# A hybrid mixer block on one core: inverses beside the other branches, key phases beside them without priority, gates beside the recurrence

## The chip, the core and the metric

The kernel runs on one core of a Trainium2 chip. The metric is the device time of one execution in microseconds. TensorE (PE in the profile) multiplies matrices, VectorE (DVE) and ScalarE (ACT) do elementwise work, GpSimd (POOL) does little but issue DMAs here, and SyncE (SP) issues the weight loads.

## The reference

One layer of a sequence model: 512 frames (`S`), width 1024, one batch. The input goes through an RMS norm and one wide projection. Its columns feed three mixers, which are gated, added and projected back; an MLP with squared ReLU and a final norm follow.

```
h = rms_norm(x, norm1_g);  p = h @ w_in
y_a = b_a * causal_dwconv(c_a * x_a)                       # short gated convolution
y_b = rg_lru(causal_dwconv(x_b)) * gelu(g_b)               # gated linear recurrence
r, decay, k, v, kk, a = ...                                # RWKV-7: keys, values, decays
state = state * w_t + (state @ -kk_t) (kk_t * a_t) + v_t k_t ;  y_t = state @ r_t
y_c = (norm(y) * lnx_g + lnx_b + bonus) * g_c
m = gate_a * y_a + gate_b * y_b + gate_c * y_c             # gates: sigmoid(p_g + bias)
x = x + m @ w_out
x = x + square(relu(rms_norm(x) @ w1)) @ w2 ;  out = rms_norm(x)
```

The third mixer has 16 heads of 64 and runs in eight chunks (`CHUNK = 64`) whose state is carried on.

## The kernel before

**Precision.** Every projection is computed from fp32 values split into a high and a low part. `load_w` fetches one 128x1024 weight block on SP's queue into `raw` (two buffers), ScalarE makes the high part `whi`, VectorE the low part `wlo`, and `mm3` (L165 to L168) does three matmuls per contraction block, 24 per block of 128 output columns (`proj`).

**Phase 1, four groups `g` of four heads.** `krv(g)` projects keys, receptances and values, builds the decays and the operands `AR` and `BK` of the chunk-internal products, and stores some of them to DRAM. `amat(g)` multiplies `BK` with `AR` for every chunk (tiles `pA`, L522), masks the products on VectorE into `AXt`, transposes `BK` (`pB`) and stores. `inverse(g)` solves a triangular system per chunk and head: 31 steps of two VectorE operations on the tiles `dg` and `Z`, with transposes ahead (L549) and behind (L566, L571), then two blocks of 32-wide matmuls (`pG`, `pT`) and the store `ttd`.

**Other branches.** `ab(q)`, for eight column blocks `q`, is mixer A and mixer B of 128 columns: eight projections, small gate matmuls (`pga`, `pgi`), ScalarE functions and a VectorE scan. It yields 32 times and stores its part of `m` to `mpd`. `gate(q)` is the third mixer's gate: the projection `gc`, the small matmul `pg2` with the low-rank gate, and the merge with `mpd` (read back as `yc` on POOL's queue).

**Phase 2, the recurrence.** `chain()` goes through eight chunks. Each has three dependent blocks of 64-wide matmuls (`pu` from the state, `pu` again with the inverse, `pS` for the next state) with copies on VectorE and ScalarE between, and the outputs `py`. `load_chunk` fetches the operands (`sv`, `ax`, `tc`, `bk`, `rt`) of the next chunk on POOL's queue into two buffers each. After every second chunk `norm` normalises two chunks of output, on VectorE for the most part.

**Phase 3.** `fin_m` transposes four chunks of output (`pYt`), multiplies them with the gate and splits the sum into `mh` and `ml`; `w_out(th)` is the output projection of one half of the frames (tiles `acc`, then `x2T`, `h2h`, `h2l`). Then come the MLP's two matrices (tiles `p` and `acc`) and the final norm.

**What sets the order.** The kernel is written in generators, and a scheduler with its own idea of durations places each engine's instructions by priority. `weave(crit, fill, r)` advances a critical generator and, after each of its steps, the filler by `r` steps on average. What the critical one emits gets a priority offset: `CP = 150` unless it yields another number (`CPI`, `CPC`, `CPN`). `pin` keeps small blocks of matmuls together on PE. In phase 1 the critical generators are `krv(0)` and `amat(0)`, and then, for each later group, `krv(g)` and `inverse(g-1)` step by step side by side, followed by `amat(g)`; the filler is `ab`. In phase 2 the chain is critical with 3.9 filler steps to each of its own; the filler is the rest of `ab`, then the gates, then `fin_m(0, 4)` and `w_out(0)`. `end()` does `fin_m(4, 8)`; what then remains of the filler, `w_out(1)` and the MLP follow.

Of the kernel before, what the change touches and what calls it, by code (L numbers as in the profile page):

```python
# [18 lines left out]
P = 128  # L19

OFF, OFFS, OFFP = 160, 20, 30
CP, CPI, CPC, CPN = 150, 60, 70, 5
HOT = 6000

NINV, NG_T = 16, 2


N_AB = 28
R0, R1, R2, R3, R4 = 0.85, 0.60, 1.25, 3.9, 1.0
NWARM = 2  # L30
POOL_KT = (1, 3, 5, 6, 7)
S = 512
# [3 lines left out]
KT = 8  # L36
NG = 4
# [59 lines left out]
def block_kernel(ctx, tc, xt, win, par, mulr, sw, wout, w1, w2, fg, cst, eyes, out):  # L97
# [415 lines left out]
    def amat(g, G_):  # L513

        G_.AX = p1.tile([P, 2, NC, 4, L], F32, tag="AXt", name="AXt")
        for c4 in range(2):
            pts = four_banks("pA")
            for i in range(16):
                ci, jj, h = i // 4, i // 2 % 2, i % 2
                c = 4 * c4 + ci  # L520
                rows = slice(64 * h, 64 * h + 64)
                pin(i, lambda: pe.matmul(pts[2 * h + jj][:, ci], G_.BK[rows, jj, c], G_.AR[rows, jj, c],  # L522
                                 start=True, stop=True))
            for e in range(4):
                tt(G_.AX[:, :, 4 * c4:4 * c4 + 4, e], pts[e].rearrange("p c (a t) -> p a c t", a=2),
                   mask.rearrange("p (a t) -> p a t", a=2).unsqueeze(2).to_broadcast([P, 2, 4, L]), MUL)
            yield
        gp.dma_start(axd[:, 0:64, g, 1].rearrange("c s e t -> s c (e t)"),
                     G_.AX[0:64, 1].rearrange("s c e t -> s c (e t)"))
        for a in range(2):  # L530
            gp.dma_start(axd[:, 64:128, g, a].rearrange("c s e t -> s c (e t)"),
                         G_.AX[64:128, a].rearrange("s c e t -> s c (e t)"))
        BKT = p1.tile([P, NC, 2, P], F32, tag="BKT", name="BKT")
        for c2, pt in enumerate(four_banks("pB")):
            for i in range(4):
                c, jj = 2 * c2 + i // 2, i % 2
                pin(c2 + i, lambda: pe.transpose(pt[:, i], G_.BK[:, jj, c].rearrange("p a t -> p (a t)"), ident))
            ac.copy(BKT[:, 2 * c2:2 * c2 + 2].rearrange("p c j t -> p (c j) t"), pt)
        gp.dma_start(bkd[:, :, g].rearrange("c p j x -> p c (j x)"), BKT.rearrange("p c j x -> p c (j x)"))
        yield  # L540

    def inverse(g, G_):
# [35 lines left out]
            ac.copy(gs[32:64, 16 * half:16 * half + 16], pg[32:64])  # L578
            yield
        for _ in range(NG_T):  # L580
            yield CPI
        for half in range(2):
            pg = pm.tile([P, 16, 32], F32, tag="pm", name="pT")
            for i in range(16):
# [31 lines left out]

    def chain():
        nxt = load_chunk(0)
        yield CPC
        for c in range(NC):  # L620
            ax, sv, tc_, rt, bk = nxt
            if c < NC - 1:
# [185 lines left out]
        for x_ in gens:  # L808
            yield from x_

    def weave(crit, fill, r):
        acc, cp = 0.0, CP
        while True:
            with tc.high_priority(offset=cp):
                c = next(crit, weave)
            if c is weave:
                break
            cp = CP if c is None else c
            acc += r
            while acc >= 1.0:  # L820
                acc -= 1.0
                next(fill, None)

    def side_by_side(*gens):
        live = list(gens)
        end = object()
        while live:
            for x_ in list(live):
                c = next(x_, end)
                if c is end:  # L830
                    live.remove(x_)
                else:
                    yield c

    M = {}
    wk_ctx = ExitStack()
    wk = wk_ctx.enter_context(tc.tile_pool(name="wk", bufs=1, side="right"))
    GS = [G() for _ in range(NG)]
    fl = chainit(*[ab(q) for q in range(6)])
    weave(chainit(krv(0, GS[0]), amat(0, GS[0])), fl, R0)  # L840
    for g in range(1, NG):
        weave(chainit(side_by_side(krv(g, GS[g]), inverse(g - 1, GS[g - 1])), amat(g, GS[g])), fl, R1)
    weave(inverse(NG - 1, GS[NG - 1]), fl, R2)
    pk_ctx.close()
    p1_ctx.close()
# [10 lines left out]

    def fill_chain():
        yield from fl
        for q in (6, 7):
            yield from ab(q)  # L860
        for q in range(KT):
            yield from gate(q)
        wk_ctx.close()
# [225 lines left out]
```

## Time and profile before

| what | us |
|---|---|
| median of 3 runs (1158.6 to 1161.83) | 1159.1 |
| the profiled execution | 1160.24 |
| its span, first to last instruction | 1158.1 |
| PE busy / DVE busy / ACT busy in it | 1073.4 / 758.3 / 484.8 |
| first inverse, from its first transpose | 107.0 |
| last transpose of the fourth inverse | 538.5 |
| first matmul of the recurrence | 564.66 |
| first matmul of the MLP | 799.4 |

The span is the profile's time from the first to the last instruction; the execution's own time is 2.1 us longer. A busy engine is not an engine at its peak: PE's matmuls are pipelined, their ends are modelled, and a matmul that waits in the pipe counts as busy. So work on PE is better counted in instructions: 90 wide matmuls of 512 columns pass in 20 us of the MLP. Counts from a trace can be a few per cent low.

### The profile page before, as it was taken

To read this page: it belongs to the slowest core of one execution; us is meant where nothing else is said; L and a number is where in the kernel's file an instruction comes from. 1 tells how busy PE (TensorE), PEld (TensorE's weight loads), DVE (VectorE), ACT (ScalarE), POOL (GpSimd) and SP (SyncE) were. 2 spreads that over 40 slices of the span, in tenths; PEclk is the share of its full clock that TensorE was granted. 3 is DMA by queue.
4 is the path that set the end of the run, shared out by engine and by line. 5 is a ranking of instruction groups with operands and counts; after the bars stand their busy time and mean duration, and the time that the engine had idled before them with its cause. 6 is when DMAs were issued, how large, how long until landed. Compare 5 with 4: busy or idle time off the path is not lost.

```text
span 1158.1 us, 16176 instructions
## 1 busy us (share of the span) xinstructions
PE 1073.4 (93%) x6396; PEld 877.3 (76%) x6396; DVE 758.3 (65%) x1300; ACT 484.8 (42%) x714; POOL 108.6 (9%) x167
## 2 busy tenths in 40 slices
PE   8899898998899788996999999969999999999997
PEld 5677676876677566785788888868888888888885
DVE  7997998599957996697375767877444444222224
ACT  6645443544345343543364644535443343121123
POOL 4211000010001000100211120000000000000001
PEclk9999898998999888897999999979999999999999
DMA  6344533362236322361865474426322334333331
GB/s 206 96 126 109 140 94 110 101 172 86 84 109 173 96 77 97 91 169 60 261 214 169 155 217 146 165 91 196 114 91 93 107 92 156 133 93 91 104 97 72
DMA packets 44475, 146.32 MB, mean 126 GB/s; under 512 B 5808, under 2 KB 9392, under 8 KB 43376
## 3 DMA queue, kind: packets, MB, share of 16 engines
q1 hardware_dynamic: 30624, 95.21, 25.9%
q0 software_dynamic: 13056, 49.03, 14.9%
q8 instruction: 50, 0.82, 0.3%
q10 hardware_dynamic: 720, 1.05, 0.2%
q14 instruction: 25, 0.20, 0.1%
HBM read 120.11 MB, written 25.17 MB: 125 GB/s over the span
## 4 chain that ended last, share of the span: by engine, by line
PE 48%; DVE 4%; DMA 3%; issue 1%; ACT 1%; POOL 0%; ACTq 0%; POOLq 0%; DVEq 0%
PE acc L167 5%; PE acc L166 5%; PE acc L168 5%; PE p L168 5%; PE p L166 5%; PE p L167 5%; PE pp L168 4%; PE pp L167 4%; PE pp L166 4%; DMA raw<-in_wout 1%; PE py L642 1%; ACT whi L145 1%; DVE wlo L102 1%; DMA raw<-in_w 1%; DMA bk<-bkd 1%
## 5 line engine op out<-in xcount | busy, mean ns | idle before, releaser
L102 DVE TENSOR_TENSOR wlo<-raw,whi 128x1024 fp32r<-128x1024 f32 (+1 forms) x172 | 209.1, 1217 | 290.6 <-ACT whi L145 289.5
L145 ACT CAST whi<-raw 128x1024 fp32r<-128x1024 f32 (+1 forms) x172 | 177.8, 1036 | 359.4 <-PE pp L167 137.3
L166 PE MATMUL pp<-hh,whi 128*128 128x512 f32 x696 | 280.1, 406 | 19.2 <-DVE ks L105 10.2
L167 PE MATMUL pp<-hl,whi 128*128 128x512 f32 x696 | 282.0, 406 | 3.2 <-DVE hl L105 3.2
L168 PE MATMUL pp<-hh,wlo 128*128 128x512 f32 x696 | 281.7, 406 | 1.9 <-DVE wlo L102 1.9
L166 PEld LDWEIGHTS pp<-hh,whi 128*128 128x128 f32 x696 | 135.8, 195 | 52.3 <-DVE ks L105 11.5
L167 PEld LDWEIGHTS pp<-hl,whi 128*128 128x128 f32 x696 | 135.6, 195 | 33.4 <-DVE hl L105 4.0
L168 PEld LDWEIGHTS pp<-hh,wlo 128*128 128x128 f32 x696 | 136.1, 196 | 31.2 <-DVE wlo L102 2.3
L168 PE MATMUL p<-h2h,wlo 128*128 128x512 f32 (+1 forms) x264 | 101.1, 383 | 0.0
L166 PE MATMUL p<-h2h,whi 128*128 128x512 f32 (+1 forms) x264 | 101.1, 383 | 0.0
L167 PE MATMUL p<-h2l,whi 128*128 128x512 f32 (+1 forms) x264 | 101.0, 383 | 0.0
L166 PE MATMUL acc<-whi,ah 128*128 128x512 f32 x256 | 99.6, 389 | 0.0
L167 PE MATMUL acc<-wlo,ah 128*128 128x512 f32 x256 | 99.6, 389 | 0.0
L168 PE MATMUL acc<-whi,al 128*128 128x512 f32 x256 | 99.6, 389 | 0.0
L167 PEld LDWEIGHTS p<-h2l,whi 128*128 128x128 f32 x264 | 49.6, 188 | 9.7
L168 PEld LDWEIGHTS p<-h2h,wlo 128*128 128x128 f32 x264 | 49.6, 188 | 9.7
L166 PEld LDWEIGHTS p<-h2h,whi 128*128 128x128 f32 x264 | 49.6, 188 | 9.5
L166 PEld LDWEIGHTS acc<-whi,ah 128*128 128x128 f32 x256 | 48.0, 188 | 10.1
L167 PEld LDWEIGHTS acc<-wlo,ah 128*128 128x128 f32 x256 | 48.0, 188 | 10.1
L168 PEld LDWEIGHTS acc<-whi,al 128*128 128x128 f32 x256 | 48.0, 188 | 9.8
L102 DVE TENSOR_TENSOR Z<-Z,dg 64x31 f32<-64x31 f32 (+15 forms) x124 | 42.2, 340 | 4.0
L102 DVE TENSOR_TENSOR dg<-Z 64x31 f32<-64x31 f32 (+15 forms) x124 | 42.2, 340 | 3.9
(296 smaller groups left out, 1479.2 us busy)
## 6 DMA issues: line engine op xcount, KB each, us to landing
raw<-in_win SPq DMA_DIRECT2D x88, 512.0 KB, 3.5
raw<-in_w SPq DMA_DIRECT2D x64, 512.0 KB, 3.5
ax<-axd POOLq DMA_DIRECT2D x8, 1024.0 KB, 8.0
raw<-in_wout SPq DMA_DIRECT2D x16, 512.0 KB, 3.5
axd<-AXt POOLq DMA_DIRECT2D x12, 512.0 KB, 7.2
bkd<-BKT POOLq DMA_DIRECT2D x4, 1024.0 KB, 13.9
bk<-bkd POOLq DMA_DIRECT2D x7, 512.0 KB, 4.5
swr<-in_sw SPq DMA_DIRECT2D x16, 128.0 KB, 2.5
```

Of the source, the lines that this page charges most:

```text
L102: return v.tensor_tensor(out=o, in0=a, in1=b, op=op)
L145: ac.copy(hi[:, sl], raw[:, sl])
L166: pe.matmul(ps, wh, xh, start=start, stop=False)
L167: pe.matmul(ps, wh, xl, start=False, stop=False)
L168: pe.matmul(ps, wl, xh, start=False, stop=stop)
L642: pin(behind, lambda: pe.matmul(py[64 * h:64 * h + 64, x], w, y, start=first and x == 0, stop=last, skip_group_check=True))
```

## The change

Phase 1 is woven in turn instead of side by side. For each later group, first `inverse(g-1)` is critical with 29 filler steps spread over its 41, then `krv(g)` with priority offset 0 and 14 filler steps over its 22, then five filler steps alone, then `amat(g)` with one filler step to each of its own. All eight `ab` are in the filler from the start. The last inverse has 0.8 filler steps to each of its own (before 1.25), the chain 1.6 (before 3.9). In `inverse` the 4 steps (before 2) between its two blocks of matmuls have priority 0; the chain's own priority goes from 70 to 20 and six steps (before one) follow the first chunk load. `amat` starts each chunk with the second head pair. No instruction is added or removed.

```diff
-CP, CPI, CPC, CPN = 150, 60, 70, 5
+CP, CPI, CPK, CPC, CPN = 150, 60, 0, 20, 5
 HOT = 6000
-NINV, NG_T = 16, 2
-N_AB = 28
-R0, R1, R2, R3, R4 = 0.85, 0.60, 1.25, 3.9, 1.0
+NINV, NG_T, N_LOAD = 16, 4, 6
+N_INV, N_KRV = 41, 22
+F_INV, F_KRV, F_GAP = 29, 14, 5
+R0, R2, R3, R4 = 0.85, 0.8, 1.6, 1.0
...
-                ci, jj, h = i // 4, i // 2 % 2, i % 2
+                ci, jj, h = i // 4, 1 - i // 2 % 2, i % 2
...
         for _ in range(NG_T):
-            yield CPI
+            yield 0
...
         nxt = load_chunk(0)
-        yield CPC
+        for _ in range(N_LOAD):
+            yield CPC
...
-    def weave(crit, fill, r):
-        acc, cp = 0.0, CP
+    def weave(crit, fill, r, base=CP):
+        acc, cp = 0.0, base
...
-            cp = CP if c is None else c
+            cp = base if c is None else c
...
-    def side_by_side(*gens):
-        live = list(gens)
-        end = object()
-        while live:
-            for x_ in list(live):
-                c = next(x_, end)
-                if c is end:
-                    live.remove(x_)
-                else:
-                    yield c
...
-    fl = chainit(*[ab(q) for q in range(6)])
-    weave(chainit(krv(0, GS[0]), amat(0, GS[0])), fl, R0)
-    for g in range(1, NG):
-        weave(chainit(side_by_side(krv(g, GS[g]), inverse(g - 1, GS[g - 1])), amat(g, GS[g])), fl, R1)
+    fl = chainit(*[ab(q) for q in range(KT)])
+    weave(krv(0, GS[0]), fl, R0)
+    for g in range(NG):
+        if g:
+            weave(inverse(g - 1, GS[g - 1]), fl, F_INV / N_INV)
+            weave(krv(g, GS[g]), fl, F_KRV / N_KRV, CPK)
+            for _ in range(F_GAP):
+                next(fl, None)
+        weave(amat(g, GS[g]), fl, 1.0)
     weave(inverse(NG - 1, GS[NG - 1]), fl, R2)
...
         yield from fl
-        for q in (6, 7):
-            yield from ab(q)
         for q in range(KT):
             yield from gate(q)
```

What this does to the order shows at three places. In the changed file the helpers' lines are one higher (L102 becomes L103).

The first place is VectorE in the middle of the first inverse. `Z` and `dg` are its own; `a`, `AR` and `BK` belong to the keys of group 1, `wlo` is a low weight part, `u` and `g` belong to the branches. Before:

```order
L102 TENSOR_TENSOR Z<-Z,dg 64x14x18
L102 TENSOR_TENSOR wlo<-raw,whi 128x1024
L105 SCALAR_TENSOR_TENSOR BK<-a_1267,a_1263 128x8x64
L108 TENSOR_SCALAR a_1270<-a_1255,part,dv 128x512
L102 TENSOR_TENSOR dg<-Z 64x255
L102 TENSOR_TENSOR a_1270<-a_1270,ks 128x512
L102 TENSOR_TENSOR Z<-Z,dg 64x15x17
L102 TENSOR_TENSOR BK<-a_1270,a_1263 128x8x64
L102 TENSOR_TENSOR dg<-Z 64x256
```

With the change:

```order
L103 TENSOR_TENSOR Z<-Z,dg 64x14x18
L103 TENSOR_TENSOR wlo<-raw,whi 128x1024
L103 TENSOR_TENSOR dg<-Z 64x255
L106 SCALAR_TENSOR_TENSOR u_1187<-u_1138,part,u_1187 128x511
L103 TENSOR_TENSOR Z<-Z,dg 64x15x17
L106 SCALAR_TENSOR_TENSOR u_1187<-u_1138,part,u_1187 128x510
L103 TENSOR_TENSOR dg<-Z 64x256
L106 SCALAR_TENSOR_TENSOR u_1187<-u_1138,part,u_1187 128x509
L103 TENSOR_TENSOR Z<-Z,dg 64x16x16
```

The key operations have left the inverse: between its first and last transposes stood 76 operations of other tiles and 11 weight splits in the first group, and now 14 and 7.

The second place is PE in the recurrence, around the second block `pu` of a chunk. `pp` is a projection (of a branch before, of a gate now), `pg` the small gate matmul. Before, in the third chunk:

```order
L167 MATMUL pp<-hl,whi 128x512
L168 MATMUL pp<-hh,wlo 128x512
L166 MATMUL pp<-hh,whi 128x512
L652 MATMUL pu<-u_5033,tc 64x64 x16
L167 MATMUL pp<-hl,whi 128x512
L168 MATMUL pp<-hh,wlo 128x512
```

With the change, in the fourth:

```order
L167 MATMUL pp<-hh,whi 128x512
L168 MATMUL pp<-hl,whi 128x512
L169 MATMUL pp<-hh,wlo 128x512
L654 MATMUL pu<-u_5433,tc 64x64 x16
L167 MATMUL pg_5466<-lgh,swch 128x512
L168 MATMUL pg_5466<-lgl,swch 128x512
L169 MATMUL pg_5466<-lgh,swcl 128x512
```

Before, 22 projection matmuls stood between that chunk's two `pu` blocks and 23 between the second and `pS`; now it is 8 and 8, and 3 of `pg`. Over the recurrence up to its last `pS` the projection matmuls go from 475 to 211, and ahead of the recurrence from 1673 to 1896.

The third place is PE at the recurrence's end. `pYt` are the transposes of `fin_m`, `acc` is the output projection. Before:

```order
L702 MATMUL pYt<-ident,Y 128x128 x4
L632 MATMUL pu<-sv,ax 64x64 x16
L642 MATMUL py<-St,rt 64x64 x16
L702 MATMUL pYt<-ident,Y 128x128 x8
L166 MATMUL acc<-mh,whi 128x256 x3
L167 MATMUL acc<-ml,whi 128x256
```

With the change, 27 matmuls after the last `py` of the last chunk:

```order
L167 MATMUL pg_6345<-lgh,swch 128x512
L168 MATMUL pg_6345<-lgl,swch 128x512
L169 MATMUL pg_6345<-lgh,swcl 128x512
L704 MATMUL pYt<-ident,Y 128x128 x12
L167 MATMUL acc<-mh,whi 128x256 x3
L168 MATMUL acc<-ml,whi 128x256
```

Before, the first half's output projection began between the last chunk's first `pu` block and its second; now all of it follows the last chunk.

## The prediction

> **What bounds the kernel now.** I read the page first, then the busy time by stretch, then the groups of instructions. The first fence is the page: totals, and the span in 40 slices of 29 us.
>
> ```profile
> span 1158.1 us, 16176 instructions
> PE 1073.4 (93%) x6396; PEld 877.3 (76%) x6396; DVE 758.3 (65%) x1300; ACT 484.8 (42%) x714; POOL 108.6 (9%) x167
> PE   8899898998899788996999999969999999999997
> DVE  7997998599957996697375767877444444222224
> PEclk9999898998999888897999999979999999999999
> ```
>
> PE at 93% looks full, but the dents of the PE row stand under the nines of the DVE row (slices 4 to 18). The second view cuts the span where the stages change. Columns: stretch, its length, then busy time (and instruction count) of PE, PEld, DVE, ACT, POOL, granted clock, DMA share, GB/s.
>
> ```profile
> 43.00:98.00 55.00, 53.78 (x239) 42.74 (x240) 47.51 (x107) 31.13 (x48) 4.85 (x8) 1.00 0.39 113
> 107.60:193.90 86.30, 75.38 (x306) 59.98 (x305) 82.28 (x155) 31.39 (x45) 8.10 (x13) 0.92 0.42 115
> 193.90:237.00 43.10, 43.10 (x346) 35.34 (x345) 26.25 (x39) 24.11 (x36) 5.35 (x9) 1.00 0.40 115
> 237.00:319.00 82.00, 71.91 (x287) 56.98 (x287) 78.13 (x151) 33.55 (x50) 7.45 (x12) 0.92 0.42 113
> 361.40:455.00 93.60, 75.00 (x304) 59.27 (x304) 85.47 (x162) 36.69 (x54) 8.02 (x13) 0.89 0.39 105
> 564.60:719.80 155.20, 155.14 (x1534) 126.71 (x1536) 99.23 (x174) 77.91 (x117) 21.29 (x39) 0.99 0.59 191
> 719.80:799.40 79.60, 67.63 (x646) 64.12 (x646) 62.12 (x128) 36.64 (x66) 6.11 (x10) 0.91 0.44 146
> 799.40:1158.10 358.70, 350.01 (x1572) 290.34 (x1570) 132.88 (x157) 114.25 (x159) 8.02 (x9) 0.99 0.33 107
> 107.00:538.50 431.50, 381.44 (x2041) 305.94 (x2039) 361.37 (x650) 184.72 (x267) 42.16 (x65) 0.93 0.41 113
> 820.00:840.00 20.00, 20.00 (x90) 16.55 (x89) 8.88 (x12) 7.63 (x11) 0.00 (x0) 1.00 0.33 106
> ```
>
> Where keys and inverse run side by side (rows two, four and five) DVE is 91 to 95% busy and PE, though shown as 80 to 87% busy, retires 304 to 306 instructions in 86 to 94 us; at the rate of the last row, 20.00/90 = 0.222 us for a 512-wide matmul, those are about 68 us of work. Between them (row three) PE is full and DVE is 61% busy. So the group section alternates between a DVE bound and a PE bound. The recurrence, 564.6 to 719.8, is bound by PE: 155.14 of 155.20. Behind it, up to the first MLP matmul at 799.4, neither is full. The last 358.7 us are the MLP, which the change leaves alone.
>
> Priced in the same way over 107.0 to 538.5 (first transpose of the first inverse to the last one of the fourth), the old PE order holds 1389 matmuls of 512 columns, 308.6 us, and small forms of 32.5 us (by the time between their starts): 341.1 us of work in 431.5 us. **90.4 us, or 21%, are lost there.** DVE, each row of its order priced at the mean of its group, has 374.6 us in it. The two ends come from these rows (first and last start):
>
> ```profile
> L549 DVE STREAM_TRANSPOSE Z<-AXt x8: 2073/2096/2107, 107.0 to 492.3; 32x1024 f32<-32x1024 f32 x8
> L571 DVE STREAM_TRANSPOSE dg<-Z x4: 1222/1226/1233, 192.7 to 538.5; 32x1024 f32<-32x1024 f32 x4
> ```
>
> **The change, stage by stage.** It removes no instruction and adds none; it only moves work, so the sum is one of stage lengths. Unit prices (line, engine, names, count, busy us, mean ns, idle before it):
>
> ```profile
> L102 DVE TENSOR_TENSOR wlo<-raw,whi 128x1024 fp32r<-128x1024 f32 x168 | 206.5, 1230 | 284.9 <-ACT whi L145 283.8
> L102 DVE TENSOR_TENSOR Z<-Z,dg 64x31 f32<-64x31 f32 (+15 forms) x124 | 42.2, 340 | 4.0
> L102 DVE TENSOR_TENSOR dg<-Z 64x31 f32<-64x31 f32 (+15 forms) x124 | 42.2, 340 | 3.9
> L145 ACT CAST whi<-raw 128x1024 fp32r<-128x1024 f32 (+1 forms) x172 | 177.8, 1036 | 359.4 <-PE pp L167 137.3
> L566 DVE STREAM_TRANSPOSE Z<-Z 32x1024 f32<-32x1024 f32 x8 | 16.1, 2016 | 0.2
> L102 DVE TENSOR_TENSOR u<-u,g 128x512 f32<-128x512 f32 x8 | 5.5, 688 | 4.5 <-ACT u L771 4.5
> L522 PE MATMUL pA<-AR,BK 64*128 64x128 f32 x256 | 22.0, 287 | 17.0 <-DVE BK L102 13.9 <-DVE AXt L102 1.8 <-DVE BK L105 0.7
> ```
>
> *Inverse stretches.* One inverse on DVE is 62 steps (84.4/4 = 21.1 us) and four transposes (2 x 2.10 + 2 x 2.02 = 8.2): 29.3 us. In the new order each of the four has branch work beside it: 7 or 8 weight splits of 1.23 and 14 to 21 other operations of about 0.69. Sums: 48.4, 52.8, 52.3, 50.9 = 204.4 us. PE has 42.2, 45.7, 46.2 and 44.9 us there, so DVE sets the length. Priced so, the old first inverse makes 84.5 us and took 85.7 (107.0 to 192.7), factor 1.01; the old last one, which already stands beside branches alone, 45.6 against 538.5 - 492.3 + 2.1 = 48.3, factor 1.06. Bounds 1.01 to 1.12; I take 1.05, near the form that is like it: **214.6**.
>
> *Keys and products* (inverse's end to the next inverse's start, three of them). PE now has 277, 266 and 285 wide matmuls there plus small ones: 70.0, 67.6, 71.8 = 209.4 us; DVE 67.3, 65.0, 67.6 = 199.9. They run without priority, but old keys of group 0 beside branches show that both engines can be full: 239 instructions, nearly all wide, x 0.222 = 53.1 us in 55.0, factor 1.04, with DVE busy for 47.5 of it. The pA row is the warning: PE stood 17.0 us at products for BK, in four groups. Bounds 0.99 (all of that pause gone by the swapped order, which now starts with the head pair finished last) to 1.13; I take 1.05: **219.9**.
>
> *Last inverse to recurrence.* The small matmuls, the store of the inverse and the first chunk load are the same chain, 538.5 to 564.6: **26.1**, bounds 24 and 28.
>
> *Recurrence to its last state product.* 475 projection matmuls become 211, 21 gate matmuls 15 and 12 convolution-gate matmuls 5: 277 fewer, 277 x 0.222 = 61.5. 155.2 - 61.5 = **93.7**, if PE stays the bound. DVE's sum there falls from 108.9 to 73.6, so it is nearer to PE than before (0.79 against 0.70), and about seven chunks of 13.4 us leave less slack. How short a chunk can be, the chain of waits shows: its first one, with little beside it, went from first product to first product in 11.0 us, so 2.4 us are left.
>
> ```profile
> 564.66 1.15 PE pu L632 x32
> 575.62 1.08 PE pu L632 x32
> raw<-in_wout SPq DMA_DIRECT2D x16, 512.0 KB, 3.5
> ```
>
> Bounds 90 (PE's work with the old 4% of waits) and 106 (13.4 and half of what a wlo or a norm step of 1.2 us adds at each of three DVE hand-overs per chunk).
>
> *Behind it, up to the MLP.* Eight tiles of output projection for the first half now come after, with two gates. PE gets 41 more projections and 6 more gate matmuls, and 6 transposes go: 60.7 to 70.5 us, +9.8. Old length 79.6. DVE's sum up to the last operand of the MLP's first half goes from 68.2 to 77.9; 79.6 x 77.9/68.2 = 90.9, by PE 79.6 x 70.5/60.7 = 92.5. I take **92**, bounds 86 and 100: all of fin_m and both projection halves stand in line on DVE, with some 12 us of PE idle (estimate: 24 of DVE work against 12 of PE) while both halves are merged. The weight loads on SP, all 16 of them now behind the chain, are no tighter bound: two buffers, each busy 3.5 us for landing and 1.04 + 1.23 for the two splits, give a tile every 2.9 us, 46 for 16.
>
> *MLP and end*: 358.7, and six transposes more: **359.4**.
>
> Sum: 107.0 + 214.6 + 219.9 + 26.1 + 93.7 + 92 + 359.4 = 1112.7 us of span. The profiled execution took 1160.24 for a span of 1158.1; the median of the runs is 1159.1, 1.0 above that span. **Forecast 1114 us**, 45 less: 61.5 leave the recurrence, 3 come back in the group section with 47.3 us more of PE work in it, and 13 come back behind the recurrence.
>
> **Rivals.**
> *Slower: PE keeps losing 21%.* If the loss in the group section is PE queued in order behind late DVE results, as the pA row has it, and not DVE's occupancy, then 388.4/0.79 = 491.6 us instead of 434.5: 1114 + 57 = 1171. Keys lose their priority, which feeds this; row one, full on both engines, speaks against it. It decides from a loss of 19%, where the section reaches 480.
>
> *Chunk loads late.* A chunk's ax is requested when the chunk two before it has ended, behind sv on POOL, and the merge loads yc of the gates stand between:
>
> ```profile
> ax<-axd POOLq DMA_DIRECT2D x8, 1024.0 KB, 8.0
> L717 POOL DMA_DIRECT2D yc<-mpd x7 | 3.8, 544 | 28.5 <-DVE bv L105 16.6 <-DVE gst L108 6.8 <-DVE swcl L102 5.1
> L605 POOL DMA_DIRECT2D sv<-vtd x6 | 3.5, 580 | 19.4 <-ACT sv L629 10.3 <-issue 7.7 <-ACT Y L674 1.3
> ```
>
> 0.58 + 0.54 + 8.0 = 9.1 us, or 13.2 with one yc wait (28.5/7 = 4.1) ahead, against 13.4 per chunk. Loads some 3 us late in each of seven chunks make 20: 1134. [...]
>
> *The clock drops in the key stretches.* It is 0.92 where PE starves now. If the pauses of PE at each inverse's end do that to the PE-bound key stretches, 219.9/0.92 = 239: 1133. [...]
>
> *Both engines full.* Inverse at 1.01 and keys at 1.00: 206.4 + 209.4, 19 less; recurrence at 90: 1091.
>
> *Nothing moves*, because the freed PE time returns elsewhere: 1159. Against it: the recurrence is PE-bound at 155.14 of 155.20 and loses 277 matmuls.
>
> **How the numbers follow.** Forecast 0.58 (its own range 1097 to 1130), slower 0.07, loads 0.12, clock 0.08, both full 0.12, nothing 0.03. 0.3% (3.5 us) is about what a measurement tells from no change. Faster: 0.58 + 0.12 + 0.08 + 0.12 = 0.90; same 0.03; slower 0.07. All bounds at once would give 1074 and 1170; for 8 in 10 I take 1088, just under both full, to 1146, above loads and clock.
>
> **What would show it.** Inverse stretches of 50 to 57 us with DVE over 92%; key stretches of about 73 us with PE near full and clock near 1.00; pA's idle under 17; first pu near 567; chunks of 13 to 14 us; first MLP matmul near 753. Wrong if key stretches pass 85 us, if PE in the recurrence waits for ax or sv, or if the part behind it passes 100.

## The result and the profile after

The changed kernel takes 1148.1 us (median of 4 runs, 1143.0 to 1152.2), the kernel before beside it 1160.5 (1158.6 to 1162.9): a ratio of 0.989, 95% interval 0.984 to 0.994. In a later comparison it took 1149.7 (6 runs) against 1160.8, ratio 0.990 (0.988 to 0.992). It is some 12 us faster, about 1%, where 45 were forecast, and 2 us above the range. The profiled execution took 1150.43 us, its span is 1148.7.

The page of the changed kernel, the lines that answer to the first fence of the prediction:

```profile
span 1148.7 us, 16170 instructions
PE 1071.1 (93%) x6396; PEld 875.9 (76%) x6396; DVE 753.9 (66%) x1300; ACT 484.2 (42%) x714; POOL 107.6 (9%) x167
PE   8899969999699996999878999789999999999997
DVE  7997967879579894898955777966544444222224
PEclk9999969999699996999979999889999999999999
```

The dents of the PE row have become narrow and regular: a 6 in the sixth, eleventh and sixteenth slice, each with a 6 in the clock row under it. The span cut by stage (columns as in the prediction) shows them between an inverse and the keys behind it. The rows are in turn: an inverse and the keys behind it three times, the last inverse, the way to the recurrence, the recurrence, the part behind it, and the MLP to the end.

```profile
106.70:157.70 51.00, 43.05 (x190) 34.85 (x187) 48.17 (x88) 17.14 (x24) 3.54 (x5) 0.94 0.46 129
157.70:244.70 87.00, 84.20 (x488) 67.30 (x489) 61.20 (x108) 40.06 (x59) 9.79 (x16) 0.90 0.35 102
244.70:300.20 55.50, 46.26 (x205) 37.48 (x203) 52.47 (x94) 23.89 (x35) 3.55 (x5) 0.95 0.42 121
300.20:384.00 83.80, 81.71 (x485) 65.78 (x486) 59.35 (x106) 42.01 (x62) 10.65 (x18) 0.91 0.36 106
384.00:439.20 55.20, 45.28 (x199) 36.74 (x197) 52.14 (x95) 23.52 (x33) 2.79 (x4) 0.93 0.46 131
439.20:525.40 86.20, 83.99 (x501) 67.76 (x502) 61.72 (x107) 40.96 (x61) 9.19 (x15) 0.93 0.37 104
525.40:579.10 53.70, 44.29 (x197) 36.31 (x195) 50.69 (x93) 23.30 (x33) 3.38 (x5) 0.96 0.42 115
579.10:606.50 27.40, 25.21 (x201) 20.68 (x202) 9.88 (x13) 8.60 (x13) 6.14 (x11) 0.83 0.53 154
606.50:701.30 94.80, 92.62 (x1287) 74.92 (x1289) 68.38 (x132) 46.42 (x73) 19.80 (x36) 1.00 0.78 252
701.30:789.50 88.20, 77.85 (x663) 72.13 (x658) 65.69 (x136) 41.06 (x73) 6.17 (x10) 0.92 0.43 138
789.50:1148.70 359.20, 350.67 (x1578) 290.90 (x1576) 133.37 (x157) 114.88 (x162) 8.56 (x10) 0.99 0.34 107
```

| term of the forecast | forecast | measured |
|---|---|---|
| to the first inverse | 107.0 | 106.7 |
| four inverse stretches | 214.6 | 51.0 + 55.5 + 55.2 + 53.7 = 215.4 |
| **three stretches of keys and products** | **219.9** | **87.0 + 83.8 + 86.2 = 257.0** |
| last inverse to recurrence | 26.1 | 27.4 |
| recurrence | 93.7 | 94.8 |
| behind it | 92 | 88.2 |
| MLP and end | 359.4 | 359.2 |

One term is 37 us off; no other is off by more than 3.8, and together the others are 1.1 us short of their forecast. The key stretches have a PE that is 97 to 98% busy at a clock of 0.90 to 0.93, and a DVE that is busy for 70 to 72%. Cut into pieces of 3.4 us, the end of the first inverse and the start of the keys read so:

```profile
148.10:151.60 3.50, 0.00 (x1) 0.00 (x0) 3.23 (x9) 1.53 (x2) 0.00 (x0) 1.00 0.19 75
151.60:155.00 3.40, 1.65 (x3) 0.83 (x3) 3.13 (x9) 0.00 (x0) 0.00 (x0) 0.50 0.47 151
155.00:158.40 3.40, 0.00 (x0) 0.00 (x0) 3.34 (x3) 0.00 (x0) 0.00 (x0) 0.50 0.01 4
...
161.80:165.20 3.40, 3.40 (x27) 2.42 (x26) 1.02 (x2) 1.98 (x3) 0.00 (x0) 0.50 0.31 125
165.20:168.60 3.40, 3.40 (x32) 2.49 (x30) 1.09 (x2) 2.52 (x4) 0.00 (x0) 0.50 0.00 0
168.60:172.00 3.40, 3.40 (x57) 3.34 (x56) 0.43 (x1) 1.59 (x4) 0.00 (x0) 0.50 0.02 5
172.00:175.40 3.40, 3.40 (x9) 2.63 (x8) 2.07 (x4) 2.62 (x5) 0.71 (x1) 0.50 0.44 125
175.40:178.80 3.40, 3.40 (x16) 2.73 (x16) 1.97 (x3) 1.04 (x3) 0.84 (x2) 0.98 0.36 70
```

Here and below, a wide matmul is one of 512 columns. PE waits while DVE ends the inverse (148.1 to 159.0, with three projections at 152), and the clock halves. Then PE is full in four pieces running and the clock stays at 0.50 until 175.5, 24 us in all. What stands there are the 32-wide blocks `pG` and `pT`, 64 matmuls each, and 20 wide ones; the last nine of these follow `pT` without a narrow one between (171.5 to 175.5), and then the clock is back. Behind the next two inverses the half clock lasts 20.5 us each. The pause has a name in the groups of instructions, first of the changed kernel, then of the kernel before:

```profile
L577 PE MATMUL pG<-dg,AXt 32*32 32x32 f32 x256 | 14.7, 236 | 36.5 <-DVE dg L572 36.5
```

```profile
  DVE dg L571: 9.0, 1
540.00:552.50 12.50, 12.50 (x141) 10.80 (x140) 5.25 (x8) 2.30 (x4) 0.71 (x1) 0.51 0.30 78
```

In the kernel before `pG` waited 9.0 us for `dg`, once: at the last inverse, the one that stood beside branches alone. There too PE was then full for 12.5 us at a clock of 0.51. Now all four inverses have that form, and the wait is 36.5.

### The profile page after: what moved, and what is told of

The parts are those of the page before. It is cut to its first block, busy times and chain, and to the rows that moved or that the text cites. A ratio compares the mean times of both kernels' runs of the same rounds, so it can differ in the third digit from the quotient of the medians.

```text
span 1148.7 us, 16170 instructions
## 1 busy us (share of the span) xinstructions
PE 1071.1 (93%) x6396; PEld 875.9 (76%) x6396; DVE 753.9 (66%) x1300; ACT 484.2 (42%) x714; POOL 107.6 (9%) x167
## 3 DMA queue, kind: packets, MB, share of 16 engines
q10 hardware_dynamic: 720, 1.05, 0.2%
## 4 chain that ended last, share of the span: by engine, by line
PE 53%; DVE 10%; issue 7%; DMA 2%; ACT 1%; POOL 1%; ACTq 0%; POOLq 0%; DVEq 0%; SPq 0%
PE acc L167 6%; PE acc L168 6%; PE acc L169 6%; PE p L168 5%; PE p L167 5%; PE p L169 5%; PE pp L167 4%; PE pp L169 4%; PE pp L168 4%; DVE wlo L103 2%; DMA rt<-rtd 2%; PE py L644 1%; DVE dg L103 1%; DVE Z L103 1%; PE pA L523 1%
## 5 line engine op out<-in xcount | busy, mean ns | idle before, releaser
L103 DVE TENSOR_TENSOR wlo<-raw,whi 128x1024 fp32r<-128x1024 f32 (+1 forms) x172 | 209.5, 1219 | 274.1 <-ACT whi L146 260.4
L167 PE MATMUL pp<-hh,whi 128*128 128x512 f32 x696 | 270.9, 403 | 4.0 <-ACT g L747 1.1
L169 PE MATMUL pp<-hh,wlo 128*128 128x512 f32 x696 | 268.7, 400 | 4.2 <-DVE wlo L103 4.2
L168 PE MATMUL pp<-hl,whi 128*128 128x512 f32 x696 | 267.9, 399 | 2.8 <-DVE hl L106 2.8
L167 PEld LDWEIGHTS pp<-hh,whi 128*128 128x128 f32 x696 | 133.3, 192 | 36.0 <-ACT hh L291 1.5
L169 PEld LDWEIGHTS pp<-hh,wlo 128*128 128x128 f32 x696 | 133.3, 192 | 34.5 <-DVE wlo L103 6.0
L577 PE MATMUL pG<-dg,AXt 32*32 32x32 f32 x256 | 14.7, 236 | 36.5 <-DVE dg L572 36.5
L103 DVE TENSOR_TENSOR dg<-Z 64x31 f32<-64x31 f32 (+15 forms) x124 | 42.2, 340 | 4.1
```

Of the source, the lines that this page charges most:

```text
L103: return v.tensor_tensor(out=o, in0=a, in1=b, op=op)
L167: pe.matmul(ps, wh, xh, start=start, stop=False)
L168: pe.matmul(ps, wh, xl, start=False, stop=False)
L169: pe.matmul(ps, wl, xh, start=False, stop=stop)
L577: pin(i, lambda: pe.matmul(pg[32:64, i], AXt[0:32, 0, l // 4, l % 4, 32:64], d1[0:32, l], start=True, stop=True))
```

## The experiments

The theory to be tested: the change puts a pause of PE at the end of each inverse, the clock halves in it and does not come back in the small blocks behind it, and this makes the key stretches long. The rivals: keys without priority come late and PE waits for them; turning keys and inverse one after the other is itself a loss; or the gain of the chain's half did not come.

### Wide matmuls ahead of the small blocks

Sixteen extra matmuls of 512 columns stand ahead of `pG`, on a bank of PSUM (the memory that matmuls write) that is free in phase 1. `zs` is the second VectorE operation of a step; the first of the sixteen waits for that of step 30.

```diff
+            if s == 30:
+                gate_ins = zs
...
+        wm = pc.tile([P, S], F32, tag="pu", name="wm")
+        for i in range(16):
+            with tc.high_priority(offset=HOT):
+                m = pe.matmul(wm, bd, hh[:, 0], start=True, stop=True)
+            if i:
+                tc.keep_in_program_order(m)
+            else:
+                tc.add_manual_dep(m.ins, gate_ins.ins.name, mybir.DependencyInfo(mybir.DependencyClass.Sync, mybir.DependencyReason.DATA), reason="warm")
         d1 = gs = dg
         v.transpose(d1[0:32], TT[0:32, :, 0:32])
```

> The change plus 16 wide matmuls (512 columns, result never read) per inverse, put on PE just ahead of the block pG, the first one held until the inverse's step 30; nothing is left out. They cost 16 x 0.222 = 3.6 us of PE each time, 14 in all, partly in PE's idle time there. As a side effect 15 to 31 projection matmuls move from ahead of pG to behind it. If the half clock at the start of the key stretches (14.3, 12 and 12 us at 0.50 in the changed kernel) is what makes them 84 to 87 us long instead of 73, the half-clock pieces behind pG vanish and the key stretches shrink by 6 to 8 us each before the displaced projections (3 to 7 us) are added; the whole is 1130 to 1145. If the clock is only a companion of late VectorE results, the key stretches stay at 84 to 87 us plus the displaced work, and the whole is 1150 to 1165.

Measured: 1148.8 us, ratio 0.990 (0.988 to 0.992). The whole lies between the two ranges, nearer to the second, but the trace fits the first theory: behind `pG` there is no half clock left in any key stretch, and the mean clock of the profiled execution is 0.970 for the change's 0.955. PE had 16 x 0.227 = 3.6 us more to do per inverse (up to twice that at half clock, where wide matmuls of the change stand 0.43 us apart, as from 172.09 to 172.52); that this and the displaced projections ate the gain is reckoned and not shown. So the next run had eight of them.

```diff
-        for i in range(16):
+        for i in range(8):
```

> As the run with 16 extra wide matmuls ahead of pG, but with 8, and only 11 to 20 projections displaced. That run had no half clock in the key stretches any more, lost 5.5 to 6.8 us of PE time in each instead of 10 to 13, and paid it back with 3.6 us of extra matmuls and 9 us of waiting ahead of them per inverse. If 8 wide matmuls (3.6 us at half clock) bring the clock back as 16 did, the whole is 1139 to 1146. If they don't, the half clock stays behind pG, and the whole is 1148 to 1156.

Measured: **1141.5 us, ratio 0.982 (0.979 to 0.986)**. The key stretches of that run, again from the first row of the last transposes to the next inverse:

```profile
159.60:241.70 82.10, 80.84 (x503) 64.60 (x502) 61.06 (x107) 41.71 (x60) 9.78 (x16) 0.99 0.39 108
297.50:381.10 83.60, 82.85 (x502) 66.13 (x502) 59.26 (x105) 41.88 (x62) 10.60 (x17) 0.96 0.38 106
436.50:520.80 84.30, 83.32 (x518) 66.47 (x516) 61.89 (x107) 42.45 (x63) 9.23 (x15) 1.00 0.38 107
```

The clock is 0.99, 0.96 and 1.00 for 0.90, 0.91 and 0.93 in the change. The sum is 250.0 us for 257.0. The extra matmuls lie ahead of these stretches, but 45 projections that stood in the inverse stretches of the change are now in them (877 wide matmuls start there, for 832): 250.0 - 45 x 0.227 = 239.8. The two profiles of the change (below) give the price of a low clock in these stretches: 0.06 more of mean clock made the same 87.0 us 5.1 us shorter, and 0.06 x 87.0 is 5.2. So I reckon the loss as the length times what the mean clock lacks to 1.00. Taking off what is still lost, 0.01 x 82.1 + 0.04 x 83.6 = 4.2, leaves 235.6. The change's own stretches less their loss, 257.0 - (0.10 x 87.0 + 0.09 x 83.8 + 0.07 x 86.2) = 257.0 - 22.3, are 234.7. So two kernels give the same length at full clock within 1 us. Of the 22.3 us this run wins back 18, and the displaced projections (10.2 us) take more than half of that again.

The 0.96 of the second stretch tells something more. The clock was back at 297.0 and halved again at 303.8, though PE never paused; what ran from 299.5 to 305.6 were `pG` and `pT` with three wide matmuls among them.

```profile
297.10:303.80 6.70, 6.70 (x110) 5.35 (x108) 2.18 (x3) 1.45 (x3) 0.00 (x0) 1.00 0.23 81
303.80:310.60 6.80, 6.80 (x45) 5.64 (x45) 0.00 (x0) 1.54 (x3) 0.72 (x1) 0.50 0.38 74
```

### Narrow matmuls in their place

Is it the time on PE, or the width? In place of the 8 wide matmuls the kernel asks for 64 of 32 by 32.

```diff
-        for i in range(8):
+        for i in range(64):
...
-                m = pe.matmul(wm, bd, hh[:, 0], start=True, stop=True)
+                m = pe.matmul(wm[32:64, 0:32], AXt[0:32, 0, 0, 0, 32:64], TT[0:32, 0, 0:32], start=True, stop=True)
```

> As the run with 8 extra wide matmuls ahead of pG (1141.5 us), but with 64 extra matmuls of 32 by 32 in their place (result never read), held by the same step of the inverse: at half clock 64 x 56 ns = 3.6 us, as long as the 8 wide ones. If only wide matmuls bring the clock back, the half clock goes on behind pG for 13 us and more as in the changed kernel, and the whole is 1147 to 1156. If any 3.5 us of uninterrupted PE work does it, the half-clock piece ends near pG and the whole is 1139 to 1146.

Measured: 1171.7 us, ratio 1.012 (1.008 to 1.015), above both expectations. Each of the 64 became two matmul instructions, 512 in the four inverses, so that the block held PE for 28.1/4 = 7.0 us and not for the 3.6 that the expectation reckoned with. These 28 us are more than the 22 to 24 by which this kernel is longer than the change, so its time says nothing of the clock; its trace does. The block in all, then the first inverse's end in two pieces:

```profile
L576 PE MATMUL wm<-Z,AXt 32*32 32x32 f32 x512 | 28.1, 236 | 39.8 <-DVE Z L569 39.8
151.40:158.00 6.60, 2.07 (x39) 2.10 (x40) 6.27 (x11) 0.00 (x0) 0.00 (x0) 0.50 0.28 82
158.00:182.20 24.20, 24.20 (x247) 20.11 (x245) 7.32 (x10) 11.35 (x18) 0.71 (x1) 0.50 0.20 48
```

PE is full for 24.2 us without a gap, and the clock stays at 0.50 to the end of it. Half of these 24.2 us are narrow matmuls (12.1 us); the other half are wide ones, in pieces of 2.4, 3.3 and 1.6 us between narrow blocks and in one of 4.8 us at the end, after which the clock is back. Behind the first three inverses the half clock lasts 30.7, 23.9 (in two pieces) and 23.9 us, against 23.9, 20.5 and 20.5 in the change. So here a busy PE did not by itself bring the clock back: narrow matmuls did not, though the block held PE for 7.0 us, nearly twice as long as the eight wide ones, and the wide ones did, with the projections behind them (4.9 us, 155.6 to 160.5).

### Real work in the same place

Wide matmuls need not be extra ones. Fourteen more steps lie ahead of `pG` in the first three inverses, their filler is taken from the key stretches, and `pG` waits in order for the last projection emitted there.

```diff
-F_INV, F_KRV, F_GAP = 29, 14, 5
+F_INV, F_KRV, F_GAP = 29, 8, 1
...
-        for _ in range(NINV):
+        for k_ in range(30 if g < NG - 1 else NINV):
             yield CPI
+            if k_ == (29 if g < NG - 1 else NINV - 1):
+                ahead = LAST[0]
...
+                if not l:
+                    tc.add_manual_dep(m.ins, ahead.ins.name, mybir.DependencyInfo(mybir.DependencyClass.Sync, mybir.DependencyReason.DATA), reason="late")
```

(`LAST[0]` is the last matmul of the projection emitted last.)

> The change with projections of the branches in the place of extra matmuls: in the first three inverses 14 more steps lie between the last step and pG, with 10 more filler steps, and pG is held behind the last projection emitted there; the key stretches have 8 and 1 filler steps in place of 14 and 5. In order this puts 22 more projections ahead of the first pG and 17 to 24 wide matmuls between pG and pT in all three (2 to 4 in the changed kernel). If wide work there is what brings the clock back, the half-clock pieces of 23.9, 20.5 and 20.5 us shrink to about 14, without the 3.6 us of extra matmuls: 1136 to 1146. If it only moves the waits, because VectorE's low weight parts come no earlier, or because the keys have less beside them, 1146 to 1158.

Measured: 1142.0 us, ratio 0.984 (0.982 to 0.987), in the middle of the first range, with no instruction added. The half clock behind the first three inverses lasts 10.2, 13.7 and 17.1 us. `pG` still waits 38.6 us for `dg`, so the pause is not what became shorter; what differs in the order is the wide matmuls behind it. Eight extra ones (`warm` issues them as above) and six such steps together:

```diff
-F_INV, F_KRV, F_GAP = 29, 14, 5
+F_INV, F_KRV, F_GAP = 29, 11, 3
...
-        for _ in range(NINV):
+        for _ in range(22 if g < NG - 1 else NINV):
             yield CPI
+        if True:
+            warm(gate_ins, 8)
```

> The run with 8 extra wide matmuls ahead of pG, and in the first three inverses 6 more steps there with the filler that goes with them, taken from the key stretches (11 and 3 filler steps in place of 14 and 5): the extra matmuls bring the clock back, the projections fill what is left of the wait. If both add up, 1134 to 1140. If the waits for VectorE are the same in either case, and only the clock counts, 1139 to 1145.

Measured: 1143.3 us, ratio 0.985 (0.983 to 0.987). They do not add up: the key stretches are at 0.99 to 1.00, but 254.6 us in sum for the 250.0 with the eight alone, with 22 projections more in them (899 wide matmuls for 877, 5.0 us). And with eight more wide matmuls per inverse, held by step 20, to keep the clock from halving at all:

```diff
+            if s == 20 and True:
+                warm(zs, 8)
...
+        if True:
+            warm(gate_ins, 8)
```

> As the run with 8 extra wide matmuls (1141.5 us), with 8 more per inverse, held by the inverse's step 20. They cost 1.8 us each time only where PE is not idle anyway; it waits some 9 us for VectorE before each pG. [...] If in-order waits move with them, they cost 4 x 1.8 us or more: 1143 to 1152.

Measured: 1148.9 us, ratio 0.991 (0.988 to 0.993). The clock halves earlier, for 3.4 to 10.2 us at a time, and the whole is 7 us longer than with eight, for 32 more wide matmuls (7.3 us). Placed so, they did not fill the pause.

### The change itself, execution by execution

> The changed kernel itself again, beside the two others on the same chip: 1145 to 1150, ratio to before 0.987 to 0.992. If the versions with a mended clock are no better than the change, all three agree within 3 us.

Measured: 1149.7 us, ratio 0.990 (0.988 to 0.992), against 0.985 and 0.985 of the two kernels beside it (with extra matmuls and steps, above; side by side, below): their intervals do not touch. Its profiled execution was one of the shortest, 1145.7 us, and its key stretches say why:

```profile
157.50:239.40 81.90, 79.19 (x487) 63.32 (x488) 60.91 (x107) 39.90 (x58) 9.78 (x16) 0.96 0.37 108
295.10:378.90 83.80, 81.83 (x484) 65.86 (x485) 59.19 (x105) 41.93 (x61) 10.56 (x17) 0.91 0.37 106
434.20:520.50 86.30, 84.08 (x502) 67.85 (x502) 61.74 (x107) 41.01 (x61) 9.23 (x15) 0.93 0.36 104
```

The same instructions as in the first profile, and the first stretch is 81.9 us at 0.96 instead of 87.0 at 0.90, the others alike: there the half clock ended after 13.7 us and not after 23.9. So 10.2 us less at half clock made the same work 5.1 us shorter: on this stretch, where PE is full, each microsecond at half clock cost half a microsecond. The lengths of the half clock here are whole multiples of 3.4 us (13.7, 20.5 and 23.9 are 4, 6 and 7 times 3.41). Counted in such pieces from where the clock halved, the two profiles differ in the place of the same seven wide matmuls between the two halves of `pG`: in this execution they nearly filled one piece (160.6 to 163.8, piece 160.4 to 163.8) and the clock was back at its end; in the first profile they lay across two (160.8 to 164.1, border at 161.9), and the clock came back only behind `pT`. That their place decided it is the author's reading of two executions; no run tests it. Over its six executions the span goes with the mean granted clock: 1143.9 us at 0.961, 1144.0 at 0.959, 1147.3 at 0.957, 1148.5 at 0.955, 1149.6 at 0.957, 1151.5 at 0.951.

### Each half of the change alone

Keys and inverse side by side again, with the chain's half kept:

```diff
-            weave(inverse(g - 1, GS[g - 1]), fl, F_INV / N_INV)
-            weave(krv(g, GS[g]), fl, F_KRV / N_KRV, CPK)
+            weave(side_by_side(krv(g, GS[g]), inverse(g - 1, GS[g - 1])), fl, 0.60)
```

> Only the chain's half of the change: keys and inverse of the groups are woven side by side again (0.60 filler steps to each), all else as in the change, so all eight branches still go ahead of the recurrence, gates beside it, output projection behind. The forecast gave the group section 434.5 us with 47 us more PE work than the 431.5 of before; the changed kernel took 472. If the side-by-side order carries the extra work as badly as it carried the old (21% lost), the section from the first inverse to the last is 341 + 47 = 388, over 0.79 = 491, and the whole is 1160 to 1172. If its VectorE-bound stretches take the extra projections into PE's idle time, it is 440 to 465 and the whole 1110 to 1140: then turning the group section one after the other is a loss, and the gain of 12 us is the chain's alone.

Measured: **1142.4 us, ratio 0.983 (0.981 to 0.986)**: faster than the change. The forecast of the second theory holds for the section (451.2 us) and comes near for the whole. That order leaves 71 projections more for behind the recurrence's start (1825 ahead of it for 1896; by the trace they run after the last chunk), so it was run with 0.66 in place of 0.60, which gives 1896.

> Keys and inverse side by side with the change's chain, as before, but with 0.66 filler steps to each of theirs in place of 0.60: exactly as many projection matmuls (1896) now lie ahead of the recurrence as in the change; in the earlier run it was 1825. If side by side loses less of PE's time at equal work, the section from first to last inverse is 460 to 468 against 472, and the whole 1138 to 1144. If that run only won by leaving 16 us of work for a place where PE had room, the section is 470 to 478 and the whole 1145 to 1152.

Measured: 1143.9 us, ratio 0.985 (0.983 to 0.987). From first inverse to last transposes, the change and then this run:

```profile
106.70:579.10 472.40, 428.79 (x2258) 346.24 (x2255) 385.73 (x685) 210.87 (x301) 42.89 (x66) 0.93 0.40 113
```

```profile
106.20:567.30 461.10, 419.76 (x2234) 337.67 (x2232) 383.76 (x682) 206.38 (x298) 43.12 (x66) 0.96 0.41 115
```

11 us less at a clock of 0.96 for 0.93; 5 of them come back on the way from the last inverse to the recurrence, which has more projections now (32.4 us for 27.4). Side by side the pieces at half clock are 3.4 to 6.8 us, and only behind the last inverse, beside branches alone, 13.6. That fits the theory: between `pG` and `pT` the order has 32 to 77 wide matmuls in the first three groups (2 to 4 in the change). Eight extra matmuls there, on the version with 0.60:

```diff
+        if g == NG - 1:
+            warm(gate_ins, 8)
```

> The run with keys and inverse side by side and the change's chain (1142.4 us), plus 8 extra wide matmuls ahead of the last inverse's pG only, where that run was at half clock for 17.0 us (552 to 569); its other half-clock pieces are 3.3 to 6.8 us. If the clock is what is left to gain there, 4 to 8 us less: 1134 to 1139. If the stretch behind the last inverse is set by its chain of small matmuls, copies and loads alone, no gain or 2 us more: 1141 to 1146.

Measured: 1142.4 us, ratio 0.985 (0.983 to 0.987): no gain. The half clock there shrinks from 17.1 to 10.2 us, but that stretch stays at 26.6 us (26.4 without). So the clock cost nothing in it; the expectation's other theory, that its chain of small matmuls, copies and loads sets it, fits.

The groups' half alone, with the chain's old settings:

```diff
-CP, CPI, CPK, CPC, CPN = 150, 60, 0, 20, 5
-NINV, NG_T, N_LOAD = 16, 4, 6
-R0, R2, R3, R4 = 0.85, 0.8, 1.6, 1.0
+CP, CPI, CPK, CPC, CPN = 150, 60, 0, 70, 5
+NINV, NG_T, N_LOAD = 16, 4, 1
+R0, R2, R3, R4 = 0.85, 0.8, 3.9, 1.0
```

> Only the groups' half: inverse and keys one after the other as in the change, all eight branches in the filler from the start, but the recurrence with its old settings (3.9 filler steps to each of its own, priority 70, one step after the first load). The stretches up to the recurrence stay within 3 us of the changed kernel's. If the recurrence and the part behind it had the forecast gain from the gates (94.8 + 88.2 = 183 us in the changed kernel), this run loses it where output projections press on the chain: the two together come to 190 to 205 and the whole to 1155 to 1170. If the two settings are worth nothing, because the work of both parts is the same, 1145 to 1151.

Measured: 1158.5 us, ratio 0.996 (0.994 to 0.998). The recurrence and the part behind it:

```profile
601.50:742.20 140.70, 134.65 (x1563) 115.36 (x1565) 100.42 (x189) 70.18 (x112) 23.52 (x42) 0.98 0.70 227
742.20:795.20 53.00, 38.27 (x391) 36.36 (x388) 36.76 (x81) 19.61 (x38) 2.73 (x5) 0.81 0.26 84
```

193.7 us together for 183.0 in the change, as expected of settings that matter. (Up to the recurrence it is 5 us shorter than the change's first profile, where 3 were allowed: its first key stretch had the shorter half clock, as in the change's second profile.) So the gain comes from the chain's half; the groups' half alone is worth 0.4%, and beside the chain's half the order one after the other costs 6 us. The halves are not pure: all of these runs keep the swap of the head pairs and the eight branches in the filler, and the swap has a worth of its own, as the next section shows.

### Priority and the order of the products

```diff
-            weave(krv(g, GS[g]), fl, F_KRV / N_KRV, CPK)
+            weave(krv(g, GS[g]), fl, F_KRV / N_KRV)
```

> The change with the keys' priority put back (offset 150 instead of 0 while they are woven); nothing else differs. If key stretches are long because key results come late on VectorE and PE stands behind them in order, VectorE gets them earlier and the key stretches fall from 84 to 87 us to 75 to 80, the whole to 1120 to 1138. If the clock or PE's own amount of work sets their length, the whole stays within 5 us of the change's 1148. If keys with priority push weight splits back, PE lacks projections and the key stretches grow: 1150 to 1165.

Measured: 1149.1 us, ratio 0.989 (0.986 to 0.991), the same as the change. The products wait 1.6 us in all for 2.1. But the parts moved: the first key stretch is 72.3 us, even below the first expectation's 75 to 80, and the way from the last inverse to the recurrence 38.8 for 27.4. Fifty-one wide matmuls have gone from the one (226 for 277) to the other. With the same reckoning as above, the three key stretches, 241.5 us with 784 wide matmuls, at clocks of 0.93, 0.94 and 0.95, are 241.5 - 14.4 + 48 x 0.227 = 238.0 us at full clock and equal work, no shorter than the 234.7 of the change. So late key results are not what makes them long. Undoing the swap of head pairs:

```diff
-                ci, jj, h = i // 4, 1 - i // 2 % 2, i % 2
+                ci, jj, h = i // 4, i // 2 % 2, i % 2
```

> The change with the products of keys starting each chunk with the first head pair again. Products wait on VectorE's BK for some 1 to 1.5 us a group in the changed kernel. If the swap matters, the products wait 5 us more per group (as they did before: 17.0 us in four groups), key stretches are 3 to 5 us longer, the whole 1158 to 1168. If it doesn't, the whole stays within 4 us of 1148.

Measured: 1155.2 us, ratio 0.994 (0.992 to 0.996), between the two expectations and some 6 us above the change, whose interval it just meets. The pause before the products, of the kernel with the change and with the swap undone:

```profile
L523 PE MATMUL pA<-AR,BK 64*128 64x128 f32 x256 | 21.1, 284 | 2.1 <-DVE BK L106 1.1 <-DVE AXt L103 0.7 <-DVE BK L103 0.2
```

```profile
L523 PE MATMUL pA<-AR,BK 64*128 64x128 f32 x256 | 21.4, 285 | 5.4 <-DVE BK L103 1.9 <-DVE BK L106 1.8 <-DVE AXt L103 0.9
```

It is 3.3 us longer in sum and not 5 per group. At full clock that run's key stretches are 240 us for the 234.7 of the change (260.9 us at 0.92, 0.93 and 0.91), so the 6 us lie there; some 3 of them are this pause, and the others were not separated.

### The low weight parts on GpSimd

If DVE binds the inverse stretches, taking its weight splits away should shorten them and end the pause.

```diff
-        tt(lo[:, sl], raw[:, sl], f(hi[:, sl]), SUB)
+        if PL_[0]:
+            PL_[1] += 1
+        if PL_[0] and PL_[1] % 1 == 0:
+            gp.tensor_tensor(out=lo[:, sl], in0=raw[:, sl], in1=f(hi[:, sl]), op=SUB)
+        else:
+            tt(lo[:, sl], raw[:, sl], f(hi[:, sl]), SUB)
```

(`PL_[0]` is set while an inverse is woven; the second run has `% 2`.)

> The change with the low weight parts of the inverse stretches (7 or 8 each, 1.23 us on VectorE) computed on GpSimd; the same operations otherwise. Inverse stretches are bound by VectorE, so they lose 8 x 1.23 = 10 us at most (51 to 55 becomes 43 to 47) if GpSimd makes a split in under about 5 us and does not slow VectorE, PE is then closer to full there (42 to 46 us of work), the idle time ahead of pG goes, and with it the half clock behind it. If that holds the whole is 1110 to 1135. If GpSimd is slow (over 6 us per split) or takes VectorE's access to memory, projections come late, and the whole is 1150 to 1180.

Measured: 1184.9 us, ratio 1.020 (1.017 to 1.024). And with every second one there:

> As the run before, with only every second of these low weight parts on GpSimd. Half the gain where a split on GpSimd costs VectorE nothing: inverse stretches 47 to 51 us, the whole 1128 to 1142. If GpSimd is slow, the loss is also about half, or none, since each GpSimd split then has twice the time: 1140 to 1160.

Measured: 1165.4 us, ratio 1.003 (1.002 to 1.005). The split on GpSimd (first run; duration in ns as smallest, median, largest) is quick enough. But the inverse stretches come to 213.8 us for 215.4, with 600 wide matmuls in them for 770, and `pG` waits 50.8 us for 36.5: the displaced projections made the other stretches longer. The inverse's operations on DVE, with a median of 372 ns, reach 5362 (in the changed kernel 423):

```profile
L151 POOL TENSOR_TENSOR wlo<-raw,whi x28: 2350/2422/2947, 94.5 to 610.3; 128x1024 fp32r<-128x1024 f32 x28
L103 DVE TENSOR_TENSOR dg<-Z x124: 189/372/5362, 115.1 to 594.4; 64x31 f32<-64x31 f32 x8, 64x60 f32<-64x60 f32 x8, 64x87 f32<-64x87 f32 x8, 64x112 f32<-64x112 f32 x8
```

The longest stood from 134.73 to 140.09, while two splits ran on GpSimd one after the other (135.13 to 139.81), and in both runs a `dg` or `Z` operation that met a split ended only after it. Operations with an input from PSUM ran on inside a split, such as four of 0.41 us that read `pb` between 241.7 and 243.1. Why the others were held up was not shown.

## Why the prediction failed

**The step that failed** is the term "keys and products": PE's work there, 209.4 us, times 1.05, made 219.9, and it took 257.0. Its factor came from group 0's keys, which have no inverse ahead of them and ran at a clock of 1.00, so the sum had nothing for the clock. Of the 37.1 us, 22.3 are half clock (0.90, 0.91 and 0.93 in the rows above), and about 15 remain at full clock (235 for 219.9).

These 15 are work that was priced too low. A wide matmul takes 0.227 us from start to start and not 0.222 (the 90 in 20 us include those cut by the window's ends), which is 828 x 0.0045 = 3.7 us. The small matmuls stand in the sum with 209.4 - 828 x 20/90 = 25.4 us. In the run with eight extra matmuls, at nearly full clock, they take 36.2 us from start to start (`pA` 14.8, `pG` and `pT` 13.8, `pB` and `pV` 7.6), 10.8 more. That makes some 224 us of work, and 224 x 1.05 is the measured 235. That the factor fits is in part luck: with 0.227, group 0's row gives 239 x 0.227 = 54.3 in 55.0, a factor of 1.01, and 3.7 of the other 11 us are the last transpose of each inverse (1.23 us), which I counted into these stretches and which PE waits for.

```profile
139.78 0.39 PE L169 MATMUL pp<-hh,wlo 128*128 128x512 f32 x1
...
146.58 0.39 PE L169 MATMUL pp<-hh,wlo 128*128 128x512 f32 x1
```

(First start and last of 31 wide matmuls in the changed kernel: 6.80/30 = 0.227.)

**The rival "the clock drops in the key stretches"** was right in its mechanism, and had 0.08. Its price was short only through the work under it: 219.9/0.92 gives 239, 235/0.92 gives 255. Its chance was short as well, and the trace of before held the reason. The last inverse there was the one in four with the new form. I read its length off for the inverse stretches (48.3 us, and that term came out at 215.4 for 214.6), but not what followed: a wait of 9.0 us before `pG`, and 12.5 us of full PE at 0.51. I kept those 26.1 us as the term up to the recurrence, where they did no harm, and did not put them behind the other three inverses, where PE is the bound. The rival itself took its 0.92 from stretches in which PE starves.

**"PE keeps losing 21%"** was wrong as a cause, though the section took 472.4 us, between the forecast's 434.5 and its 491.6: with their priority back the keys are no shorter at equal work and clock, and the pause at the products fell from 17.0 to 2.1 us, under the 17 that was named. **"Chunk loads late"** did not decide: PE is busy for 92.62 of 94.80 us in the recurrence, with 1.3 us of waits for `ax` and 0.7 for `rt`:

```profile
L634 PE MATMUL pu<-sv,ax 128*64 128x64 f32 (+1 forms) x224 | 8.7, 225 | 2.1 <-DMA ax<-axd 1.3 <-ACT whi L146 0.9
L644 PE MATMUL py<-St,rt 64*64 64x64 f32 x192 | 6.9, 221 | 0.7 <-DMA rt<-rtd 0.7
```

**Right were** the inverse stretches (51 to 55.5 us with DVE at 94%), the recurrence (94.8 for 93.7), the part behind it (88.2 for 92) and the MLP. Of the signs named ahead, key stretches near 73 us with the clock near 1.00, the first `pu` near 567 (606.5) and the first MLP matmul near 753 (789.5) failed; "wrong if key stretches pass 85 us" is what came about. Chunks took 11.6 to 16.2 us, for 13 to 14.

## What to carry to other kernels

Where a stretch bound by another engine ends in a wait of PE (some 9 us at each inverse here) and small matmuls follow, reckon with half clock behind it (here 20.5 to 23.9 us in all; behind the first inverse it ended with nine wide matmuls that stood together, 171.5 to 175.5), and look in the old profile for a place that already has the new form, together with the stage that follows it. Half clock cost nothing here where PE was not the bound (26.6 us for 26.4 with 6.9 us less of it), and half of its length where it was (5.1 us for 10.2); an order that mixes wide matmuls into such ends was worth more (1143.9 us) than one that separates the bounds (1149.7 beside it). Putting wide matmuls there, eight extra ones or projections that are due anyway, is a cheap test (1141.5 and 1142.0 us here). Price small matmuls from start to start as well: here they were 10.8 us of the miss.

## What was not expected of the hardware

- Small matmuls did not bring the clock back: PE was full for 24.2 us at 0.50, half of it 32-wide matmuls and the rest wide ones in pieces of 1.6 to 4.8 us; eight matmuls of 512 columns with the projections behind them brought it back (4.9 us, 155.6 to 160.5). Nor did they hold it: in the run with eight it halved at 303.8 us while PE was full (6.70 of the 6.70 us before).
- One kernel's time varied with it: the same stretch took 87.0 us at 0.90 and 81.9 at 0.96, and executions of the change spread over 7.6 us of span as the mean clock went from 0.961 to 0.951.
- GpSimd operations with two inputs (2.42 us each) held up DVE operations of 0.4 us: one behind two of them took 5.36 us, while DVE operations that read PSUM ran on (0.41 us).
